# Attention scores of a hybrid decoder layer: fp32 products replaced by three products of (hi, lo) pairs

## The chip, the core and the metric

The kernel runs on one core of one Trainium2 chip. The metric is the device time of the whole program in microseconds (us). Work is spread over TensorE (PE in the profile; its weight loads have a row of their own, PEld), VectorE (DVE), ScalarE (ACT), GpSimd (POOL) and the DMA queues of SyncE (SP) and POOL.

## What is computed

One layer of a decoder trunk, 512 tokens of 1024 channels, all in fp32. Cut to the part that matters here:

```
h = RMSNorm(x);  [u | q | k | v] = h @ w_in            # 512 channels each
y_pool = pooling mixer on u, 4 groups, windows 2/4/8/16
# attention: 8 heads of 64 channels, blocks of 256 keys, top-3 past blocks + own block
l = q_head @ k_head.T * 64**-0.5 + bias(t - s);  l = where(allowed, l, -inf)
y_attn = softmax(l) @ v_head
x += RMSNorm(concat[y_pool, y_attn] @ w_out)
x += RMSNorm(conv-gated MLP of RMSNorm(x))             # 1024 -> 2 x 2816 -> 1024
x += (p @ w_ple) * sigmoid(x @ w_ple_gate)
```

With 512 tokens there are two blocks, so every past block is among the top three and the attention is plain causal attention.

## The kernel before, in words

Nearly all matrix products are done on pairs: an fp32 array is split into hi (rounded to the type fp32r) and lo (the rest, also fp32r), and a product is the sum of three fp32r matmuls into one bank, lo x hi, hi x lo and hi x hi. The helper `mm3` (lines 192 to 194) issues the three; `split` (lines 197 and 198) makes a pair, hi by an ACT copy and lo by a DVE subtraction. The class `_Weights` loads weights by SP's queue into two raw buffers and splits them into six pairs (lines 124 and 125), a few chunks ahead of their use, in the order that the program names them.

Two kinds of product are not on pairs. The transposes are fp32 matmuls against an identity. And the attention scores (`scores`, line 395) are plain fp32 matmuls: `query(hp)` and `key(hp)` project two heads at a time into one [128, 512] bank, lines 0 to 63 for the even head and 64 to 127 for the odd one, and ACT alone copies the bank to an fp32 tile, scaled by -1/8 for the queries (lines 380 and 385). For each head, `scores(h)` then issues four matmuls over the 64 lines of the head, one for each block of 128 queries, with 512, 384, 128 and 256 keys as moving columns (block i sees the keys up to its own end). They fill three banks with the tag `s`. DVE adds the bias and takes the minimum (line 401), ACT does the exponentials with the row sums (line 403), DVE scales by the reciprocals (lines 404 and 407).

The engines work their queues in program order (the schedule is manual). The attention part is one loop over the heads: some fills (a projection of 24 matmuls, or a small product `mix` of the pooling mixer, three matmuls), then `transposes(h)` (ten transposes of the softmax of head h, line 422; their three banks are split into the pair PT by ACT and DVE, lines 197 and 198), `scores(h + 1)`, and `values(h)` (eight fp32r matmuls, line 442, which read PT and V). So on TensorE the scores of the next head stand between the transposes of this head and its values, and the split of PT has the time of the scores to be done. After the last head's scores the fill is `out_part(0, 0)`, 15 matmuls of the output projection, and then `transposes(7)`.

POOL does the sums of the pooling mixer, small statistics, and issues its own DMAs: the bias table (`scr`, line 341, then `T`, line 483, which line 401 reads), gains, x, and later blocks of w_down.

The last line of the build creates the program with the default size of the ring in which POOL's DMAs put their descriptors (16384 bytes of each partition).

Of the kernel before, what the change touches and what calls it, by code (L numbers as in the profile page):

```python
# [17 lines left out]
F32 = mybir.dt.float32  # L18
F32R = mybir.dt.float32r
AF = mybir.ActivationFunctionType  # L20
ALU = mybir.AluOpType
# [3 lines left out]
P = 128  # L25
S = 512
# [5 lines left out]
DH = 64  # L32
# [107 lines left out]
def hybrid_layer(ctx, tc, x, p, rel_bias, g_mix_pre, g_mix_post, g_ffn_pre, g_ffn_post, w_in, w_pool,  # L140
                 pool_scale, w_out, w_up, conv_w, conv_b, w_down, w_ple, w_ple_gate, onehot, out):
    nc = tc.nc
    act, dve, pool, pe, sp = nc.scalar, nc.vector, nc.gpsimd, nc.tensor, nc.sync
# [10 lines left out]
    def bank(name, tag="mm"):  # L154
        return psum.tile([P, 512], F32, tag=tag, name=name, bufs=banks[tag])
# [34 lines left out]
    def mm3(o, st, mv, first, last, more=False):  # L190

        pe.matmul(o, st[1], mv[0], start=first, stop=False, skip_group_check=more)  # L192
        pe.matmul(o, st[0], mv[1], start=False, stop=False, skip_group_check=more)  # L193
        pe.matmul(o, st[0], mv[0], start=False, stop=last, skip_group_check=more)  # L194

    def split(pair, src):
        act.copy(pair[0], src)
        dve.tensor_sub(pair[1], src, pair[0].bitcast(F32))  # L198
# [77 lines left out]
    rows = early.tile([4 * NF + 4, P], F32, name="rows")  # L276
# [66 lines left out]
    ps = bank("rows", "pt")  # L343
# [12 lines left out]
    ap2 = at.enter_context(tc.tile_pool(name="attn2", bufs=1, reuse_waits="tile"))  # L356
# [10 lines left out]
    def project(name, tag="mm", n=3):  # L367
        w = W.take()
        ps = bank(name, tag)
        for k in range(KD):  # L370
            mm3(ps, [q[:, k, :] for q in w], h_moving(k), k == 0, k == KD - 1)
        W.ahead(n)
        return ps

    qT, kT, L = {}, {}, {}

    def query(hp):
        ps = project(f"q{hp}")
        qT[hp] = ap2.tile([P, S], F32, tag="qT", name=f"qT{hp}", bufs=2)
        act.mul(qT[hp], ps, -(DH ** -0.5))  # L380

    def key(hp):
        ps = project(f"k{hp}")
        kT[hp] = ap2.tile([P, S], F32, tag="kT", name=f"kT{hp}", bufs=2)
        act.copy(kT[hp], ps)

    place = {3: (0, 0, 768), 2: (1, 0, 384), 0: (1, 384, 0), 1: (2, 0, 128)}

    def scores(h):
        hp, e = divmod(h, 2)  # L390
        rows = slice(e * DH, (e + 1) * DH)
        bk = [bank(f"s{h}_{b}", "s") for b in range(3)]
        for i, (b, c, _) in place.items():
            n = (i + 1) * P
            pe.matmul(bk[b][:, c:c + n], qT[hp][rows, i * P:n], kT[hp][rows, :n], start=True, stop=True)  # L395
        L[h] = ap2.tile([P, 1280], F32, tag="L", name=f"L{h}", bufs=1)
        m = small.tile([P, 12], F32, tag="m", name=f"m{h}", bufs=2)
        for i, (b, c, o) in place.items():
            n = (i + 1) * P
            l = L[h][:, o:o + n]  # L400
            dve.tensor_tensor_reduce(out=l, in0=bk[b][:, c:c + n], in1=T[:, h, S - n:], scale=1.0, scalar=MASKED,
                                     op0=ALU.add, op1=ALU.min, accum_out=m[:, i:i + 1])
            act.activation(l, l, AF.Exp, bias=m[:, i:i + 1], scale=-1.0, accum_out=m[:, 4 + i:5 + i])
        dve.reciprocal(m[:, 8:], m[:, 4:8])
        for i, (b, c, o) in place.items():
            l = L[h][:, o:o + (i + 1) * P]
            dve.tensor_scalar_mul(l, l, m[:, 8 + i:9 + i])
# [78 lines left out]
    def y_stationary(t, k):  # L486
        return [q[:, k, t * P:(t + 1) * P] for q in yT]

    yb = {}
    part = (4, 5, 0, 1, 6)  # L490
    query(0)
    query(1)
    key(0)
    key(1)
    split(wp, wpool)
    scores(0)
    fills = {0: [lambda: pool_in(0)], 1: [lambda: pool_in(1)],
             2: [lambda: query(2), lambda: pool_out(0)],
             3: [lambda: query(3), lambda: key(2), lambda: pool_out(1)],
             4: [lambda: key(3)], 5: [lambda: pool_in(2)],  # L500
             6: [lambda: pool_in(3)]}
    after = {1: lambda: pool_mid(0), 2: lambda: pool_mid(1), 6: lambda: pool_mid(2)}
    for h in range(H - 1):
        for f in fills[h]:
            f()
        transposes(h)
        scores(h + 1)
        values(h)
        if h in after:
            after[h]()  # L510
# [77 lines left out]
    for k in range(2):  # L588
        ps = bank(f"trp{k}", "pt")
# [121 lines left out]
    for fb in range(1, NF // 2):  # L711
        for post in (gate_post, value_post):
            for f in (2 * fb, 2 * fb + 1):
                ps = project(f"{post.__name__[:4]}{f}", tags[u % 5])
# [162 lines left out]
```

## Time and profile before

| | us |
|---|---|
| median of 3 runs | 609.24 (608.72 to 611.42) |
| the profiled execution | 606.27 |
| its span, first to last instruction | 604.5 |
| TensorE busy in the span | 596.9 (99%) |
| VectorE, ScalarE, GpSimd busy | 397.9, 280.2, 180.6 |
| mean granted TensorE clock | 0.999 |

The span is the time from the first to the last instruction of the profiled execution; the execution's own time is 1.77 us longer. The profiled execution is 2.97 us faster than the median of the three timed runs, so a sum made against the trace is carried over to the median as a difference. A matmul's duration in the profile reaches beyond the start of the next one, since matmuls overlap in the array; what a matmul costs the engine is read from the starts of neighbours.

### The profile page before, as it was taken

How to read it: one execution, taken by the hardware profiler on the slowest of the kernel's cores; microseconds unless marked ns; L12 is line 12 of the kernel's file. 1: busy time of each engine (PE TensorE's matmuls, PEld its weight loads, DVE VectorE, ACT ScalarE, POOL GpSimd, SP SyncE). 2: the span in 40 equal slices, each digit the busy share in tenths (PEclk: the TensorE clock that was granted, in tenths of full speed). 3: DMA queues.
4: the chain of work that ended last, by engine and by line, in shares of the span. 5: the costliest groups of instructions: out<-in, count | busy, mean ns of one | idle time of the engine just before them, and what ended most of it. 6: DMA issues, size and time to landing. Idle time of an engine off the chain costs nothing.

```text
span 604.5 us, 7363 instructions
## 1 busy us (share of the span) xinstructions
PE 596.9 (99%) x2800; PEld 490.0 (81%) x2800; DVE 397.9 (66%) x552; ACT 280.2 (46%) x457; POOL 180.6 (30%) x198
## 2 busy tenths in 40 slices
PE   8999999999999999999999999999999999999997
PEld 5788777777888988888888888888888788888876
DVE  4732665777478668857766874654787786787432
ACT  5532655664454434413432342442565666657320
POOL 2300230045215446565646944214310000002000
PEclk9999999999999999999999999999999999999999
DMA  8676203023560696686777534224174577661311
GB/s 291 196 254 226 70 3 107 30 71 105 190 223 6 225 332 214 246 304 222 265 279 275 212 139 141 70 81 128 69 244 157 194 258 248 209 223 51 105 53 53
DMA packets 56492, 102.36 MB, mean 169 GB/s; under 512 B 2963, under 2 KB 32495, under 8 KB 55048
## 3 DMA queue, kind: packets, MB, share of 16 engines
q1 hardware_dynamic: 48344, 67.71, 34.1%
q0 software_dynamic: 8112, 34.17, 14.9%
q8 instruction: 22, 0.36, 0.3%
q14 instruction: 14, 0.11, 0.1%
HBM read 86.12 MB, written 18.37 MB: 173 GB/s over the span
## 4 chain that ended last, share of the span: by engine, by line
PE 94%; DMA 2%; DVE 1%; ACT 1%; issue 1%; SPq 1%; DVEq 0%; ACTq 0%
PE gate L192 6%; PE valu L192 6%; PE valu L194 6%; PE gate L194 6%; PE gate L193 6%; PE valu L193 6%; PE d L192 6%; PE d L194 5%; PE d L193 5%; PE s L395 3%; PE y L192 2%; PE y L193 2%; PE y L194 2%; PE g L193 2%; PE g L194 2%; PE g L192 2%
## 5 line engine op out<-in xcount | busy, mean ns | idle before, releaser
L125 DVE TENSOR_TENSOR wl<-raw,wh 128x1024 fp32r<-128x1024 f32 (+1 forms) x120 | 149.4, 1252 | 35.0 <-ACT wh L124 34.4
L124 ACT CAST wh<-raw 128x1024 fp32r<-128x1024 f32 (+1 forms) x120 | 120.6, 1021 | 24.4 <-DMA raw<-in_w_down 7.5
L679 POOL TENSOR_TENSOR b<-b 128x512 f32<-128x512 f32 x44 | 67.4, 1541 | 12.3 <-DMA b<-in_w_down 10.5
L192 PE MATMUL gate<-hT,wl 128*128 128x512 f32 x160 | 62.3, 389 | 0.0
L193 PE MATMUL gate<-hT,wh 128*128 128x512 f32 x160 | 62.3, 389 | 0.0
L194 PE MATMUL gate<-hT,wh 128*128 128x512 f32 x160 | 62.2, 389 | 0.0
L192 PE MATMUL valu<-hT,wl 128*128 128x512 f32 x160 | 62.2, 389 | 0.0
L193 PE MATMUL valu<-hT,wh 128*128 128x512 f32 x160 | 62.2, 389 | 0.0
L194 PE MATMUL valu<-hT,wh 128*128 128x512 f32 x160 | 62.2, 389 | 0.0
L192 PE MATMUL d<-wh,ml 128*128 128x512 f32 x154 | 60.0, 390 | 0.6 <-DVE ml L198 0.6
L194 PE MATMUL d<-wh,mh 128*128 128x512 f32 x154 | 59.9, 389 | 0.0
L193 PE MATMUL d<-wl,mh 128*128 128x512 f32 x154 | 59.9, 389 | 0.0
L618 ACT ACTIVATE c<-gate,cols 128x512 f32<-128x512 f32 x20 | 15.5, 777 | 67.7 <-PE gate L194 67.7
L619 DVE SCALAR_TENSOR_TENSOR c<-gate,cols,c 128x511 f32<-128x511 f32 x20 | 15.0, 748 | 36.3 <-ACT c L618 36.2
L631 ACT ACTIVATE sq<-sq 128x512 f32<-128x512 f32 x22 | 13.9, 632 | 50.2 <-DVE sq L630 50.2
L463 POOL TENSOR_TENSOR u<-u 128x512 f32<-128x512 f32 x10 | 11.3, 1134 | 80.8 <-ACT u L459 80.4
L194 PEld LDWEIGHTS gate<-hT,wh 128*128 128x128 f32 x160 | 30.0, 188 | 6.3
L194 PEld LDWEIGHTS valu<-hT,wh 128*128 128x128 f32 x160 | 30.0, 188 | 6.3
L193 PEld LDWEIGHTS valu<-hT,wh 128*128 128x128 f32 x160 | 30.0, 188 | 6.2
L192 PEld LDWEIGHTS valu<-hT,wl 128*128 128x128 f32 x160 | 30.0, 188 | 6.2
L193 PEld LDWEIGHTS gate<-hT,wh 128*128 128x128 f32 x160 | 30.0, 188 | 6.2
L192 PEld LDWEIGHTS gate<-hT,wl 128*128 128x128 f32 x160 | 30.0, 188 | 6.2
(200 smaller groups left out, 1286.0 us busy)
## 6 DMA issues: line engine op xcount, KB each, us to landing
raw<-in_w_up SPq DMA_DIRECT2D x22, 1024.0 KB, 5.3
b<-in_w_down POOLq DMA_DIRECT2D x22, 512.0 KB, 5.4
tsum<-b POOLq DMA_DIRECT2D x11, 1024.0 KB, 4.2
raw<-tsum SPq DMA_DIRECT2D x20, 512.0 KB, 5.1
raw<-in_w_down SPq DMA_DIRECT2D x15, 512.0 KB, 5.4
raw<-in_w_in SPq DMA_DIRECT2D x6, 1024.0 KB, 8.4
raw<-in_w_out SPq DMA_DIRECT2D x4, 1024.0 KB, 5.0
raw<-in_w_ple_gate SPq DMA_DIRECT2D x4, 1024.0 KB, 5.1
```

Source lines behind the costliest of these rows:

```text
L124: self.nc.scalar.copy(pair[0], view)
L125: self.nc.vector.tensor_sub(pair[1], view, pair[0].bitcast(F32))
L192: pe.matmul(o, st[1], mv[0], start=first, stop=False, skip_group_check=more)
L193: pe.matmul(o, st[0], mv[1], start=False, stop=False, skip_group_check=more)
L194: pe.matmul(o, st[0], mv[0], start=False, stop=last, skip_group_check=more)
L395: pe.matmul(bk[b][:, c:c + n], qT[hp][rows, i * P:n], kT[hp][rows, :n], start=True, stop=True)
L463: pool.tensor_tensor(out=nxt[:, 16:], in0=src[:, 16:], in1=src[:, 16 - (1 << lvl):16 + S - (1 << lvl)], op=ALU.add)
L618: act.activation(c0, pg, AF.Identity, bias=cw[:, 3, f:f + 1], scale=cw[:, 2, f:f + 1])
L619: dve.scalar_tensor_tensor(c0[:, 1:], pg[:, :S - 1], cw[:, 1, f:f + 1], c0[:, 1:], op0=ALU.mult, op1=ALU.add)
L631: act.activation(sq, sq, AF.Tanh)
L679: pool.tensor_tensor(out=b[:, o, :], in0=b[:, i0, :], in1=b[:, i1, :], op=ALU.subtract)
```

## The change

Queries and keys are split into (hi, lo) pairs when they leave PSUM: ACT still writes hi (now fp32r), and DVE gets one more instruction for each of the four query tiles (line 381 of the changed kernel) and each of the four key tiles (line 198, through `split`). `scores` calls `mm3` on the 64 lines of the head, so that each of its four matmuls becomes three fp32r ones. The pairs need twice the room of the single tiles (four tags of two buffers, 2 KB of each partition apiece), and the descriptor ring is set to 4096 bytes of each partition.

```diff
     def query(hp):
         ps = project(f"q{hp}")
-        qT[hp] = ap2.tile([P, S], F32, tag="qT", name=f"qT{hp}", bufs=2)
-        act.mul(qT[hp], ps, -(DH ** -0.5))
+        hi, lo = qT[hp] = [ap2.tile([P, S], F32R, tag=f"q{c}", name=f"q{c}{hp}", bufs=2) for c in "hl"]
+        act.mul(hi, ps, -(DH ** -0.5))
+        dve.scalar_tensor_tensor(lo, ps, -(DH ** -0.5), hi.bitcast(F32), op0=ALU.mult, op1=ALU.subtract)
 
     def key(hp):
         ps = project(f"k{hp}")
-        kT[hp] = ap2.tile([P, S], F32, tag="kT", name=f"kT{hp}", bufs=2)
-        act.copy(kT[hp], ps)
+        kT[hp] = [ap2.tile([P, S], F32R, tag=f"k{c}", name=f"k{c}{hp}", bufs=2) for c in "hl"]
+        split(kT[hp], ps)
...
             n = (i + 1) * P
-            pe.matmul(bk[b][:, c:c + n], qT[hp][rows, i * P:n], kT[hp][rows, :n], start=True, stop=True)
+            mm3(bk[b][:, c:c + n], [q[rows, i * P:n] for q in qT[hp]], [q[rows, :n] for q in kT[hp]], True, True)
...
-    nc = bacc.Bacc("TRN2", target_bir_lowering=False, num_devices=1)
+    nc = bacc.Bacc("TRN2", target_bir_lowering=False, num_devices=1, dynamic_dma_scratch_size=4096)
```

In the order of TensorE the change shows where a head's scores stand, between the transposes of the head before (pt) and that head's values (o). These are the rows before, at the scores of head 3; s are the score banks, kT and qT the key and query tiles:

```order
L422 MATMUL pt_2_811<-ident,L_725 128x128 x3
L395 MATMUL s_0_817<-kT_544,qT_480 128x512
L395 MATMUL s_1_818<-kT_544,qT_480 128x384
L395 MATMUL s_1_818<-kT_544,qT_480 128x128
L395 MATMUL s_2_819<-kT_544,qT_480 128x256
L442 MATMUL o_839<-PT_409,V 128x512
```

And these are the rows of the changed kernel at the scores of head 4 (kh, kl, qh, ql are the pairs; its lines after 381 are one further down):

```order
L423 MATMUL pt_2_987<-ident,L_866 128x128 x3
L192 MATMUL s_0_993<-kh_964,ql_823 128x512
L193 MATMUL s_0_993<-kl_965,qh_822 128x512
L194 MATMUL s_0_993<-kh_964,qh_822 128x512
L192 MATMUL s_1_994<-kh_964,ql_823 128x384
L193 MATMUL s_1_994<-kl_965,qh_822 128x384
L194 MATMUL s_1_994<-kh_964,qh_822 128x384
L192 MATMUL s_1_994<-kh_964,ql_823 128x128
L193 MATMUL s_1_994<-kl_965,qh_822 128x128
L194 MATMUL s_1_994<-kh_964,qh_822 128x128
L192 MATMUL s_2_995<-kh_964,ql_823 128x256
L193 MATMUL s_2_995<-kl_965,qh_822 128x256
```

Four matmuls of a head have become twelve, in the same place; nothing else on TensorE has moved.

On VectorE the added subtraction of the last key tile stands directly ahead of the split of PT on which the values of head 4 wait. Before (wl is the lo half of a weight chunk):

```order
L451 TENSOR_TENSOR yT_89<-d_981,t_978 64x512
L125 TENSOR_TENSOR wl_1010<-raw_788,wh_1009 128x1024
L198 TENSOR_TENSOR PT_409<-pt_0_1015,PT_408 128x512
L198 TENSOR_TENSOR PT_409<-pt_1_1022,PT_408 128x384
L198 TENSOR_TENSOR PT_409<-pt_2_1028,PT_408 128x384
```

Now:

```order
L452 TENSOR_TENSOR yT_89<-d_1035,t_1032 64x512
L125 TENSOR_TENSOR wl_1064<-raw_820,wh_1063 128x1024
L198 TENSOR_TENSOR kl_1068<-k_1038,kh_1067 128x512
L198 TENSOR_TENSOR PT_409<-pt_0_1071,PT_408 128x512
L198 TENSOR_TENSOR PT_409<-pt_1_1078,PT_408 128x384
L198 TENSOR_TENSOR PT_409<-pt_2_1084,PT_408 128x384
```

One instruction has come in ahead of the three splits.

## Rows read from the trace of the kernel before

**Rows 1.** The page's first part (busy us of each engine, share of the span, instructions) and the row of the granted TensorE clock in 40 slices, in tenths of full speed.

```profile
PE 596.9 (99%) x2800; PEld 490.0 (81%) x2800; DVE 397.9 (66%) x552; ACT 280.2 (46%) x457; POOL 180.6 (30%) x198
...
PEclk9999999999999999999999999999999999999999
```

**Rows 2.** The waits of TensorE's matmuls over the whole span: what waited, for what, us in total, times, longest. The view has four more rows: one of 1.4 us at the very start, before the first weights have come, and three of 0.3 us and less.

```profile
PE d L192 <- DVE ml L198: 0.6, 1, 0.6
PE tr L233 <- DVE hT L198: 0.4, 1, 0.4
```

**Rows 3.** The timeline of TensorE's matmuls from the last transposes of head 0 through the scores of head 1 to the first two values of head 0. Columns: start, us until the last of the row has ended, engine, line, operation, out<-in, shape, how many the row takes together. The rows come from narrow windows, so the counts overlap: a row's start is that of its first matmul.

```profile
68.60 0.27 PE L422 MATMUL pt<-ident,L 128*128 128x128 f32 x1
...
68.81 0.69 PE L395 MATMUL s<-kT,qT 64*128 64x512 f32 x1
...
69.34 0.91 PE L395 MATMUL s<-kT,qT 64*128 64x512 f32 x2
...
69.77 0.81 PE L395 MATMUL s<-kT,qT 64*128 64x384 f32 x2
...
70.41 0.60 PE L395 MATMUL s<-kT,qT 64*128 64x128 f32 x3
...
70.63 0.59 PE L395 MATMUL s<-kT,qT 64*128 64x256 f32 x2
...
70.85 0.38 PE L395 MATMUL s<-kT,qT 64*128 64x256 f32 x1
...
71.16 0.50 PE L442 MATMUL o<-PT,V 128*128 128x512 f32 x1
...
71.50 0.58 PE L442 MATMUL o<-PT,V 128*128 128x512 f32 x2
```

**Rows 4.** The timeline of TensorE's weight loads in the same stretch, with the same columns; in brackets, the idle time before the row.

```profile
68.80 0.29 PEld L395 LDWEIGHTS s<-kT,qT 64*128 64x128 f32 x2 [0.17 <-issue]
69.34 0.19 PEld L395 LDWEIGHTS s<-kT,qT 64*128 64x128 f32 x1 [0.24 <-issue]
```

**Rows 5.** The timeline of TensorE's matmuls at the values of head 7, which follow a product of the pooling mixer and not scores. All of them are fp32r: two with 512 columns (the rows begin with the second of them), then two with 384, then four with 256.

```profile
150.82 0.56 PE L442 MATMUL o<-PT,V 128*128 128x512 f32 x2
...
151.04 0.33 PE L442 MATMUL o<-PT,V 128*128 128x384 f32 x1
...
151.22 0.46 PE L442 MATMUL o<-PT,V 128*128 128x384 f32 x2
...
151.39 0.52 PE L442 MATMUL o<-PT,V 128*128 128x256 f32 x3
...
151.51 0.52 PE L442 MATMUL o<-PT,V 128*128 128x256 f32 x3
```

**Rows 6.** The timeline of TensorE's matmuls from the last transpose of head 7 to the second matmul of the output projection that follows.

```profile
146.35 0.27 PE L422 MATMUL pt<-ident,L 128*128 128x128 f32 x1
...
146.69 0.39 PE L193 MATMUL y<-wl,yT 128*128 128x512 f32 x1
```

**Rows 7.** The timelines of ACT, DVE and PE around the third key tile (`key(2)`): its copy out of PSUM, a result of the mixer on DVE, the DVE part of the split of PT, the scores of head 4 and the first values of head 3.

```profile
105.14 0.59 ACT L385 COPY kT<-k 128x512 f32<-128x512 f32 x1 [3.91 <-PE k L194]
...
106.54 0.75 DVE L480 SCALAR_TENSOR_TENSOR yT<-mix,cols,yT 128x512 fp32r<-128x512 f32 x1 [4.05 <-ACT yT L479]
107.21 1.61 DVE L198 TENSOR_TENSOR PT<-pt,PT 128x512 fp32r<-128x512 f32 x3
...
106.80 2.42 PE L395 MATMUL s<-kT,qT 64*128 64x512 f32 x8
109.16 0.50 PE L442 MATMUL o<-PT,V 128*128 128x512 f32 x1
```

**Rows 8.** The same around the fourth key tile (`key(3)`): its copy on ACT, the DVE part of the split of PT, the first values of head 4.

```profile
116.22 0.59 ACT L385 COPY kT<-k 128x512 f32<-128x512 f32 x1 [2.17 <-PE k L194]
...
117.33 1.62 DVE L198 TENSOR_TENSOR PT<-pt,PT 128x512 fp32r<-128x512 f32 x3 [1.34 <-ACT PT L197]
...
119.56 0.74 PE L442 MATMUL o<-PT,V 128*128 128x512 f32 x2
```

**Rows 9.** The timelines at the last head: the DVE scaling of its softmax, the last matmul of `out_part(0, 0)`, and the weight loads of `transposes(7)` from the second on.

```profile
143.41 1.95 DVE L407 TENSOR_SCALAR L<-L,m 128x512 f32<-128x512 f32 x4
...
144.96 0.39 PE L194 MATMUL y<-wh,yT 128*128 128x512 f32 x1
...
145.41 0.42 PEld L422 LDWEIGHTS pt<-ident,L 128*128 128x128 f32 x4 [0.31 <-DVE L L407]
```

**Rows 10.** DVE at head 0: the split of the mixer's weights ahead of the softmax, the first bias row, the scaling.

```profile
60.92 0.69 DVE L198 TENSOR_TENSOR wp<-wpool,wp 128x512 fp32r<-128x512 f32 x1 [3.78 <-ACT wp L197]
61.53 0.68 DVE L401 CUSTOM_DVE_ANT_0 L<-s,T 128x512 f32<-128x512 f32 x1
...
64.80 1.27 DVE L407 TENSOR_SCALAR L<-L,m 128x512 f32<-128x512 f32 x4
```

**Rows 11.** PE at the start of `transposes(0)`, and two of the page's DMA issues of POOL's queue: KB of one, us from issue to landing; then the issue of the second on POOL's timeline.

```profile
67.62 0.38 PE L422 MATMUL pt<-ident,L 128*128 128x128 f32 x2
...
scr<-line POOLq DMA_DIRECT2D x1, 2560.0 KB, 16.6
...
T<-scr POOLq DMA_DIRECT2D x1, 2048.0 KB, 9.9
...
40.59 0.95 POOL L483 DMA_DIRECT2D T<-scr  x1 [14.87 <-DMA scr<-line]
```

## The prediction

> **What bounds the kernel now.** I read the page's first part first. TensorE is busy 99% of the span, its clock is at full speed in every slice, and VectorE, the next engine, has a third of the span free [rows 1]. A busy TensorE could still be one that waits between matmuls, so I read its waits next. Apart from the start of the program the longest is 0.6 us, in the down projection, and in the whole attention part no matmul's start is put down to another engine [rows 2]. So a microsecond less of TensorE's own work in that part is a microsecond of the whole, unless something off the engine then ends last. The question is thus what one head's scores cost TensorE now, what twelve fp32r products will cost, and at which head another engine stands close behind.
>
> For the first part I read the timeline by starts. From the first score matmul to the first matmul of the values it is 68.81 to 71.16, 2.35 us [rows 3]; it is 106.80 to 109.16 at head 4 [rows 7], and the same at the other heads. Each fp32 product appears as two records. One record takes 0.43 us for 512 columns (69.34 to 69.77), 0.32 for 384 (69.77 to 70.41 for two), 0.11 for 128 (70.41 to 70.63 for two) and 0.22 for 256 [rows 3]. That is some 1,280 columns, twice, at two clock periods of 2.4 GHz each, 2.13 us. The remaining 0.2 us stands at the ends. The first record takes 0.53 instead of 0.43, and the last one 0.31 (70.85 to 71.16) instead of 0.22 [rows 3].
>
> **What the change removes and adds on TensorE.** An fp32r matmul of the same width is a single record: 0.22 us for 512 columns (150.82 to 151.04), 0.175 for 384 (151.04 to 151.39 for two), 0.12 for 256 (151.39 to 151.51) [rows 5]. The first one after the scores takes 0.34 (71.16 to 71.50) [rows 3]: 0.12 more, for a weight load that nothing covers. I take that for the first product of the scores too, since their first record carries a like surcharge now, and I leave the 0.09 at the end, since 64 lines give way to 128 there as before.
>
> No row shows an fp32r matmul with 128 columns. The bounds are 0.06, half of the 256-column one, and 0.22, if the narrow one cost as much as the two records of the fp32 product. I take 0.11: two weight loads that follow each other without a matmul between them start 0.10 apart (0.29 us for the two, 0.19 for one [rows 4]), each product loads weights anew, and so a product cannot follow faster than that, however narrow it is. It is also what one fp32 record of this width takes.
>
> One head's scores are then 0.34 + 2 x 0.22 for 512 columns, 3 x 0.175 for 384, 3 x 0.11 for 128, 3 x 0.12 for 256, and 0.09 at the end: 2.085 us instead of 2.35. That is **0.265 us less for each head**: three passes for four, of which the narrow products and the fixed part of each instruction take half back.
>
> **What it adds elsewhere, and what covers it.** DVE gets eight more instructions: four like the mixer's from PSUM, 0.75 us [rows 7], and four subtractions of 512 columns at 0.69 [rows 10], some 5.8 us in all, beside DVE's 206 us of idle time. ACT has the same instructions as before. What matters is who waits for them, and there are three places.
>
> At the third key tile the copy on ACT ends at 105.73. The lo half takes DVE until about 106.45; DVE was idle until 106.54, and the product that reads it is the second of head 4's scores, from 106.80 on [rows 7]. It costs nothing; the cover is 0.35 us, and any lateness beyond that is paid in full.
>
> At the fourth key tile the lo half runs from about 116.84 to 117.53, directly ahead of the split of PT, which began at 117.33 [rows 8]. The split is pushed by 0.2 and ends at 119.15 instead of 118.95. The values of head 4 began at 119.56 and will want to begin at 119.30, and they need only the first third of the split at their start (about 118.2). At head 3 the split ends at 108.82 and the values will come at 108.90 [rows 7]. So the shorter scores still cover the split; about 0.9 us would have to go before the first values wait.
>
> At head 0 the second key tile pushes the mixer's split, and with it the softmax, by about 0.2 us: its scaling ends at 66.3 instead of 66.07 [rows 10], and the transposes will come at 67.35 instead of 67.62 [rows 11]. A full projection of 5.4 us covers this, as at every head but the last.
>
> At the last head this cover is 15 matmuls, 3.4 us, and it is used up: the scaling on DVE ends at 145.36, TensorE was free at 145.19, and the second transpose's load already waited until 145.41 [rows 9]. DVE's chain to that point starts from the split of PT of the head before and not from the scores (its first bias step stands right behind that split in DVE's order), so it does not get shorter. TensorE will come 0.265 us earlier and wait as much longer. **Head 7 gives nothing**, and the sum is 7 x 0.265 = 1.85 us.
>
> The larger pairs and the smaller ring move the tiles in SBUF, which changes for which released tiles POOL's loads of x and w_down wait. I cost this at nothing, as TensorE shows no wait for any of them [rows 2]. The ring itself matters for two DMAs. The bias goes through `scr` (16.6 us from issue to landing) and `T` (issued at 40.59, 9.9 us), so T has landed at 50.5 [rows 11], and DVE first reads it at 61.53 [rows 10]. A ring that slowed these would have 11 us to use up first. I cost it at nothing as well.
>
> **The sum.** The profiled execution takes 606.27 us, 1.77 of it outside the span; 606.27 - 1.85 = 604.4. That execution is 2.97 us faster than the median of the runs, so against the median it is 609.24 - 1.85 = **607.4 us**, 0.3% less. About 0.5% (3.05 us) is what a measurement of this kernel can tell from no change, so I call this no change.
>
> **The rivals.** *Narrow products at the rate of the wide ones* (0.06 us): 0.15 more for each head, 0.415 x 7 = 2.9 us, 606.3. For it: the 256-column products come near the rate of their columns. Against it: the 0.10 between two loads. If the last head's chain also gave way, it would be 3.3 us.
>
> *The ends go away.* If the surcharges at both ends (0.09 of idle time and 0.12 of uncovered load, twice) belonged to fp32 and not to the 64 lines, another 0.42 us would go from each head: 0.685 x 7 = 4.8 us, 604.4. Against it: where fp32 transposes over 128 lines give way to fp32r ones, the second of these starts 0.34 after the last transpose [rows 6], which is 0.11 + 0.23 and no surcharge.
>
> *The products are not what they say.* If the 128-column ones cost 0.22, a head takes 0.065 more than now, and 7 of them 0.5 us: 609.7. If every product over 64 lines cost an fp32 record, a head would take 3 x (0.43 + 0.32 + 0.11 + 0.22) + 0.2 = 3.45, 1.1 more, and eight heads 8.8 us: 618.0. Against the latter: the same type runs at 0.22 over 128 lines [rows 5].
>
> *Weight loads come into the open*, which ends on the other side. The place is the twelve products of a head, which all use the same 64 lines of the array. If each load stood between its neighbours as the first one does, 12 x 0.12 would come on top of the streams, 3 x (0.22 + 0.175 + 0.12 + 0.06), and 0.09: 3.25 us, 0.9 more than now, and 7.2 us for eight heads: 616.4. It decides from the third uncovered load of a head on, since each costs 0.12 and the gain is 0.265. Against it: in the scores of now the loads start with the matmul ahead of them (69.34 in both views), and a matmul follows the next one after exactly its columns [rows 3, 4]. The Trainium skill, "TensorE: Matmul & The Clock Gate", Part 3 (The mechanism), says of packed matmuls that a weight load overlaps with matmuls in flight only where the two address different rows of the array; by that rule the time would be this rival's 616.4 us, and the trace, with loads over the same 64 lines hidden behind 0.43 us records, does not agree.
>
> *The ring delays the bias.* If both DMAs took twice as long, T would land at 77.0, and head 0's softmax, 15 us late with 1 us to spare, would cost some 14 us: 623. It would have to be slower by 11 us before it cost anything.
>
> **How the numbers follow.** The forecast has 0.67, narrow products at full rate 0.13, ends that go 0.04, products that cost more 0.09 (0.07 the narrow ones, 0.02 all), open loads 0.04, the ring 0.03. The range goes from 605.6 to 609.9: it takes in the first and the narrow part of the third rival and, below, the half microsecond by which the fastest run before lies under its median. It leaves out 0.13. Faster by over 0.5% are the ends, and the part of the first rival that the last head or the spread takes over the line: 0.08. Slower by over 0.5% are all products at the fp32 price, open loads and the ring: 0.09. The rest, 0.83, is within 0.5%.
>
> **What would show it.** In the profile after, the scores of a head should take 2.0 to 2.15 us from their first start to the first values, with starts 0.22 to 0.23, 0.17 to 0.18, about 0.11 and 0.12 apart. The second transpose of head 7 should wait some 0.5 us for DVE instead of 0.3, and no other new wait of TensorE should exceed 0.2. DVE's busy time should rise by 5 to 6 us, ACT's not. The prediction is wrong if the 128-column products are far from 0.11 apart, if a load of the scores starts after the matmul ahead of it has ended, or if a wait for DVE appears ahead of head 4's scores or of any head's values.

## The result and the profile after

The changed kernel takes **605.3 us** (median of 5 executions, 604.84 to 605.99) beside 609.24 (607.21 to 611.42) for the kernel before in the same session: a ratio of 0.9935 [0.9907, 0.9963]. The forecast was 607.4, and its range ended 0.3 us higher than the result. The two profiled executions are 604.84 and 606.27 us (spans 603.1 and 604.5), so the traces account for 1.43 us, not for the 3.9 us between the medians. Where the other 2.5 us are is the main question of the experiments. The forecast called the change no change; the interval of the ratio ends below 1, so it is one, of 0.4 to 0.9%.

The first part of the page after, to be read against [rows 1]: TensorE has 1.9 us less to do, DVE 12 us more, where 5 to 6 were forecast. The eight new instructions take 0.69 us each, 5.5 in all, as forecast; the rest lies in instructions that the change doesn't touch, and DVE's busy time differs as much between profiles of one kind (397 to 404 us in the six with fp32 scores, 404 to 410 in the seven with all three products).

```profile
PE 595.0 (99%) x2832; PEld 494.5 (82%) x2832; DVE 410.0 (68%) x560; ACT 279.9 (46%) x457; POOL 184.3 (31%) x198
```

TensorE's waits over the whole span after (columns as in [rows 2]). The second row is new; it stands at the transposes of head 7.

```profile
PE d L192 <- DVE ml L198: 0.7, 1, 0.7
PE pt L423 <- DVE L L408: 0.5, 1, 0.5
PE tr L233 <- DVE hT L198: 0.4, 1, 0.4
```

TensorE's timeline after at the scores of head 1, which answers to [rows 3]; columns as there.

```profile
68.60 0.50 PE L192 MATMUL s<-kh,ql 64*128 64x512 f32 x1
68.94 0.39 PE L193 MATMUL s<-kl,qh 64*128 64x512 f32 x1
69.17 0.39 PE L194 MATMUL s<-kh,qh 64*128 64x512 f32 x1
69.41 0.33 PE L192 MATMUL s<-kh,ql 64*128 64x384 f32 x1
...
69.93 0.22 PE L192 MATMUL s<-kh,ql 64*128 64x128 f32 x1
69.99 0.27 PE L193 MATMUL s<-kl,qh 64*128 64x128 f32 x1
70.10 0.27 PE L194 MATMUL s<-kh,qh 64*128 64x128 f32 x1
70.21 0.33 PE L192 MATMUL s<-kh,ql 64*128 64x256 f32 x1
70.39 0.28 PE L193 MATMUL s<-kl,qh 64*128 64x256 f32 x1
70.51 0.28 PE L194 MATMUL s<-kh,qh 64*128 64x256 f32 x1
70.71 1.09 PE L443 MATMUL o<-PT,V 128*128 128x512 f32 x4
```

Read by starts: 0.34 for the first product, 0.23 for the next two, 0.17 for each with 384 columns, 0.06, 0.11 and 0.11 for those with 128, then 0.17 (70.21 to 70.39; the rows are rounded), 0.12 and 0.20 up to the values. The scores of a head take 2.11 us (68.60 to 70.71) in place of 2.35.

TensorE's weight loads in the same stretch (columns as in [rows 4]): the load for the second 384-column product starts at 69.41, with the matmul ahead of it, and the others likewise or 0.05 to 0.11 later; only the first load of the head (68.60) starts together with its own matmul and not ahead of it.

```profile
68.60 0.18 PEld L192 LDWEIGHTS s<-kh,ql 64*128 64x128 f32 x1 [0.17 <-issue]
...
69.41 0.18 PEld L193 LDWEIGHTS s<-kl,qh 64*128 64x128 f32 x1
...
69.93 0.18 PEld L193 LDWEIGHTS s<-kl,qh 64*128 64x128 f32 x1
70.04 0.19 PEld L194 LDWEIGHTS s<-kh,qh 64*128 64x128 f32 x1
70.15 0.19 PEld L192 LDWEIGHTS s<-kh,ql 64*128 64x128 f32 x1
```

Set against the trace before, the values of head 0 start 0.45 us earlier (71.16 to 70.71) and those of head 6 2.01 us earlier (140.36 to 138.35): 0.26 from head to head, of which 0.24 stand in the scores themselves and the rest between them. Behind head 7's transposes only 1.50 us are left (the first product there, 146.37 to 144.87). Half a microsecond is given back at that one place. Two timelines show how, DVE's of the kernel before around the splits of PT of heads 5 and 6:

```profile
127.73 1.16 DVE L198 TENSOR_TENSOR PT<-pt,PT 128x512 fp32r<-128x512 f32 x2 [1.88 <-ACT PT L197]
...
132.53 2.21 DVE L407 TENSOR_SCALAR L<-L,m 128x512 f32<-128x512 f32 x4
...
136.22 2.36 DVE L125 TENSOR_TENSOR wl<-raw,wh 128x1024 fp32r<-128x1024 f32 x2
138.61 0.69 DVE L198 TENSOR_TENSOR PT<-pt,PT 128x512 fp32r<-128x512 f32 x1
```

and the same after, with TensorE at the transposes of head 7 under it:

```profile
126.23 1.62 DVE L198 TENSOR_TENSOR PT<-pt,PT 128x512 fp32r<-128x512 f32 x3 [1.52 <-ACT PT L197]
...
131.03 2.20 DVE L408 TENSOR_SCALAR L<-L,m 128x512 f32<-128x512 f32 x4
...
134.71 2.36 DVE L125 TENSOR_TENSOR wl<-raw,wh 128x1024 fp32r<-128x1024 f32 x2
137.10 1.16 DVE L198 TENSOR_TENSOR PT<-pt,PT 128x512 fp32r<-128x512 f32 x2
...
141.90 1.91 DVE L408 TENSOR_SCALAR L<-L,m 128x512 f32<-128x512 f32 x4
```

```profile
142.96 0.40 PE L194 MATMUL y<-wh,yT 128*128 128x512 f32 x1
143.83 1.29 PE L423 MATMUL pt<-ident,L 128*128 128x128 f32 x10 [0.47 <-DVE L L408]
144.87 0.48 PE L192 MATMUL y<-wh,yT 128*128 128x512 f32 x1
```

The split of head 5 is the last thing on DVE that waits for TensorE (1.88 and 1.52 us of idle time ahead of it, ended by ACT's half of the split, which reads the transposes); it comes 1.50 us earlier. From there to head 7's scaling DVE waits only for ACT's exponentials, whose own inputs come from DVE, and every row of it comes 1.50 or 1.51 us earlier, no more: the split of head 6 stands behind two weight splits that keep DVE busy until 138.58 (now 137.07), whenever TensorE is done. So neither head 7's shorter scores nor head 6's reach the end: six heads count, not seven.

### The profile page after: what moved, and what is told of

The parts are those of the page before. It is cut to its first block, busy times and chain, and to the rows that moved or that the text cites. A ratio compares the mean times of both kernels' runs of the same rounds, so it can differ in the third digit from the quotient of the medians.

```text
span 603.1 us, 7432 instructions
## 1 busy us (share of the span) xinstructions
PE 595.0 (99%) x2832; PEld 494.5 (82%) x2832; DVE 410.0 (68%) x560; ACT 279.9 (46%) x457; POOL 184.3 (31%) x198
## 4 chain that ended last, share of the span: by engine, by line
PE 93%; DVE 3%; ACT 2%; issue 1%; POOL 1%; DVEq 0%; POOLq 0%
PE gate L192 6%; PE valu L194 6%; PE gate L194 6%; PE valu L192 6%; PE gate L193 6%; PE valu L193 6%; PE d L192 6%; PE d L193 5%; PE d L194 5%; PE g L193 2%; PE g L194 2%; PE y L194 2%; PE y L192 2%; PE g L192 2%; PE y L193 2%; PE tr L233 2%
## 5 line engine op out<-in xcount | busy, mean ns | idle before, releaser
L125 DVE TENSOR_TENSOR wl<-raw,wh 128x1024 fp32r<-128x1024 f32 (+1 forms) x120 | 152.7, 1279 | 22.7 <-ACT wh L124 22.1
L680 POOL TENSOR_TENSOR b<-b 128x512 f32<-128x512 f32 x44 | 71.2, 1628 | 10.5 <-DMA b<-in_w_down 8.8
L222 POOL TENSOR_SCALAR rd<-msd 128x1 f32<-128x1 f32 x4 | 3.1, 784 | 106.5 <-ACT M L217 106.5
```

The source lines that it names most:

```text
L125: self.nc.vector.tensor_sub(pair[1], view, pair[0].bitcast(F32))
L222: pool.tensor_scalar(r, ms, add, None, op0=ALU.add)
L680: pool.tensor_tensor(out=b[:, o, :], in0=b[:, i0, :], in1=b[:, i1, :], op=ALU.subtract)
```

## The experiments

The kernels ran in three sessions (e, g, h), each on one chip and beside runs of the kernel before, whose medians there were 607.33 (35 executions), 607.15 (20) and 607.37 (19), with 606.18 and 611.38 as the extremes. Ratios are to these runs, with their 95% intervals; they are not the ratios of the medians.

**The base, the ring, the tiles (e1 to e4).** e1 is the kernel before and e4 the changed one, unedited. e2 has one line of the change, e3 the changed kernel with a ring of twice the size, which moves its tiles again:

```diff
 e2 (kernel before)
-    nc = bacc.Bacc("TRN2", target_bir_lowering=False, num_devices=1)
+    nc = bacc.Bacc("TRN2", target_bir_lowering=False, num_devices=1, dynamic_dma_scratch_size=4096)
 e3 (changed kernel)
-    ... dynamic_dma_scratch_size=4096)
+    ... dynamic_dma_scratch_size=8192)
```

> The kernel before, unchanged, against itself: what its own executions spread over, with the span and clock of each. If the 2.5 us that the change gained beyond the 1.4 us of the two traces lie in the measurement of the kernel before (chance of the chip or the moment), its median comes out near its trace, 606 to 607, here. If they belong to the program, its executions lie at 607 to 611 again, ratio 1.00, and a trace of a slow one shows where the 1 to 5 us stand.

> The kernel before with the ring at 4096 bytes and nothing else: fp32 scores, all tiles 12 KB lower. Theory A (the scores alone act, the rest is spread): same as before, 607 to 611, scores 2.35 us a head. Theory B (ring or place of the tiles removes slow executions): 606.0 to 606.8, 2.5 us less than before, with no difference in the scores. Theory C (the ring costs something that the scores hide): above before by 0.5 us or more.

> The changed kernel with a ring of 8192 bytes, all tiles 4 KB higher than in the change. If the size of the ring acts, the time lies between: 606 to 608. If only the scores act, or the place of the tiles does not matter, it is the change's 605.3 within 0.6 us. Scores 2.11 us a head either way.

> The changed kernel unchanged, on the same chip as the three others, so that they can be compared: 604.8 to 606.0 as at first, ratio 0.9935 if the kernel before has its slow executions here too, 0.9975 (1.4 to 1.8 us) if it has not.

| | median us (12 executions) | lowest, highest | ratio |
|---|---|---|---|
| e1, before | 607.43 | 606.16, 610.7 | 0.9992 [0.9969, 1.0015] |
| e2, ring alone | 606.95 | 606.12, 608.17 | 0.9982 [0.9964, 1.0] |
| e3, pairs, ring 8 KB | 606.83 | 605.62, 607.84 | 0.9973 [0.9951, 0.9995] |
| e4, the change | 605.61 | 604.8, 605.99 | 0.9956 [0.9937, 0.9975] |

With more executions the median of the kernel before is 607.3, not 609.24, and the change is worth 1.7 us between medians (by the interval of the ratio 1.5 to 3.8). e2 lies between the ranges of its theories A and B. The executions of the kernel before are not one level with noise: of the 35, seven lie at 606.2 to 606.6, seven at 610.4 to 611.3, and the rest in steps between, while e4 stays within 1.2 us. The profiled execution of e1 (608.18) shows one of the steps. Its rows of SP's issue of a w_up block, of ACT's cast of it, and of the transposes of the second norm on TensorE:

```profile
165.74 0.37 SPq L101 DMA_DIRECT2D raw<-in_w_up  x1
...
173.88 1.05 ACT L124 CAST wh<-raw 128x1024 fp32r<-128x1024 f32 x1 [5.43 <-DMA raw<-in_w_up]
...
184.32 1.10 PE L233 MATMUL tr<-ident,h2n 128*128 128x128 f32 x8 [1.86 <-DVE h2n L570]
```

The block is issued as in the other trace of this kernel (165.83), but is cast 2.5 us later than there:

```profile
171.38 1.05 ACT L124 CAST wh<-raw 128x1024 fp32r<-128x1024 f32 x1 [2.84 <-DMA raw<-in_w_up]
```

The cast stands in ACT's queue ahead of squares (line 217) that the second norm needs, so a late block delays the norm and in the end TensorE, by 1.86 us. Up to there e1 is as early as the first trace, so this wait is all of its distance. What is in flight just ahead of that block are POOL's loads of x and p, 2.5 MB. In the kernel before they wait for the last product of the mixer; after the change the first of these tiles lies elsewhere and waits for the values of head 7 (the second gain's DMA, before and after):

```profile
156.55 0.53 POOL L211 DMA_DIRECT2D g_ffn_pre<-in_g_ffn_pre  x1 [9.38 <-PE mix L194]
157.07 1.05 POOL L538 DMA_DIRECT2D x<-in_x  x2
```

```profile
150.84 0.53 POOL L211 DMA_DIRECT2D g_ffn_pre<-in_g_ffn_pre  x1 [4.93 <-PE o L443]
151.36 1.05 POOL L539 DMA_DIRECT2D x<-in_x  x2
```

In e2 they are issued from 152.9 on and no execution is above 608.2; in e3 from 158.5 on, the second-norm transposes wait 0.6 us again, and the median is 1.2 above e4. (That wait is not all of it: see the starts below.)

**The tiles without the scores, and the scores without the early loads (g1, g2).** g1 gives the fp32 tiles the size of the pairs and takes the small ring; g2 puts the loads of the changed kernel back behind the last mixer product.

```diff
 g1 (kernel before, ring 4096)
-        qT[hp] = ap2.tile([P, S], F32, tag="qT", name=f"qT{hp}", bufs=2)
+        qT[hp] = ap2.tile([P, 2 * S], F32, tag="qT", name=f"qT{hp}", bufs=2)[:, :S]
...
 g2 (changed kernel)
+    hold = small.tile([P, 1], F32, tag="hold", name="hold", bufs=1)
+    pool.tensor_copy(out=hold, in_=yT[1][:, 3, :1].bitcast(F32))
     g_pre = gains(op_, g_ffn_pre, "g_ffn_pre")
```

> The kernel before with the ring of 4096 bytes and with query and key tiles of twice the size, of which only the first half is used: every tile and every DMA descriptor stands where the changed kernel has it, and the scores are still fp32. If the scores alone made the change (0.25 us less for each of seven heads), the executions of this kernel lie as the changed kernel's do, 1.4 to 1.8 us higher: about 606.4 and 607.3, median 606.9, none above 608.5, with x issued at 151 to 155 us and no wait of the h2n transposes for DVE. If the place of the tiles made the change, it comes to 605.6 to 606.0. If neither the ring nor the tiles do anything, it lies as before: median 607.3, a fifth of the executions above 610.

> The changed kernel with POOL's loads of the second gain, x and p held behind the last product of the mixer by a one-column copy of its result, as they stood before. If these loads, by delaying the first w_up block, make the slow executions, x is issued after 155.5 us, the cast of that block starts later than 170.5, the h2n transposes wait 0.5 to 2 us for DVE, and executions above 606.5 appear: median 606.0 to 607.0. If the moment of these loads does not matter, it lies as the changed kernel: 604.8 to 606.0, median 605.6. The scores stay at 2.11 us a head in both.

g1: 606.58 (606.22 to 608.28, 10 executions); x is issued at 152.77, no wait of these transposes shows, nothing is above 608.5. g2: 606.84 (606.13 to 607.73, 10), with 0.9981 [0.996, 1.0002]; seven of ten executions lie above 606.5. These medians jump between steps, and the ratio of g1 alone, 1.0003 [0.9993, 1.0013], shows no gain. So I take the means of all executions of a kind together (the interval is a bootstrap over them; sessions on different chips are pooled):

| | x from 151 to 153 us on | x from 157 us on |
|---|---|---|
| fp32 scores | e2, g1: 606.89 (606.61 to 607.20), 22 executions, none above 608.28 | before, e1: 607.89 (607.60 to 608.21), 86, of which 25 above 608.3 and 14 above 610 |
| pairs | the change: 605.54 (605.34 to 605.74), 23, none above 606.64 | e3, g2: 606.76 (606.47 to 607.07), 22, none above 607.84 |

Between the means, the scores are worth 1.1 to 1.35 us, and the column with the early loads, of which the diff says nothing, lies 1.0 to 1.2 lower (in medians, e2 0.4 and g1 0.6 below the kernel before). That these 1.0 to 1.2 belong to the loads is not shown, for the means hold something else as well: executions of one kernel differ from the first 20 us on. By 22 us TensorE is 1.1 us behind the first trace of the changed kernel in e4 and 2.0 in e3, and 2.0 behind the first trace of the kernel before in h2 (the kernel before with an edit at head 7, below). The scores of head 0 in the kernel before and in h2:

```profile
59.68 2.42 PE L395 MATMUL s<-kT,qT 64*128 64x512 f32 x8
```

```profile
61.57 1.77 PE L395 MATMUL s<-kT,qT 64*128 64x512 f32 x4
```

No load at 151 us can have caused this. Added to 606.2, the lowest time of the kernel before, it gives 607.3 and 608.2. Around these two, from 606.7 to 608.4, lie 47 of the 86 executions and 12 of the 22 of e2 and g1. That they are slow starts is an estimate from these three traces. e3's profiled execution is 2.71 us behind the changed kernel's first trace: 2.01 by 22 us, 0.7 at the transposes. What speaks for the loads is the tail: 23 of the 86 executions lie above 608.4, none of the 45 with early loads. Against it: none of the 22 of e3 and g2, with late loads, is above 607.84 (609.2 with the 1.4 us of the scores added), while 14 of the 86 are above 610. The late loads alone have not brought back executions as slow as these.

A size missed in g2: the transposes wait 0.25 us in its profile, not 0.5 to 2 (the cast starts at 172.21, as expected late). Of the 2 us by which that execution is slower than the one profiled of the changed kernel, 0.81 is already there at 21 us, 0.4 comes at these transposes, and some 0.5 comes between 150 and 180 us, where its 512-column products follow 0.233 instead of 0.229 apart; for that no cause was found.

**A larger dose (h1).** The kernel before, with the loads of x and p moved behind POOL's first `s` of the output projection.

```diff
-    for t in range(NT):
-        pool.dma_start(X[t], x[t * P:(t + 1) * P, :])
...
-    pool.dma_start(pin, p.rearrange("(t q) c -> q t c", q=P))
...
         s0.append(s)
+        if t == 0:
+            for i in range(NT):
+                pool.dma_start(X[i], x[i * P:(i + 1) * P, :])
+            pool.dma_start(pin, p.rearrange("(t q) c -> q t c", q=P))
```

> The kernel before with POOL's loads of x and p issued one small POOL instruction later, behind the first sum of the output projection's squares: about 163 to 166 us instead of 157 to 160. If the slow executions of the kernel before come from these 2.5 MB delaying the w_up block that is loaded at 165.8, the delay is now the rule: the cast of that block starts at 174 us or later in every execution, the h2n transposes wait 2 us or more for DVE, and the median is 608.5 to 612, with no execution under 607.5. If the executions at 610 to 611 (granted clock 0.997) are such a wait together with a late rise of the clock at the start, executions at that level come up in a third or more. If the moment of these loads does not matter, it lies as before: 606.2 to 611.4, median 607.2.

613.53 (611.38 to 614.71, 6 executions), 1.0079 [1.0054, 1.0103], a little above the range expected. In its profile the loads are issued from 164.06 to 167.1, and the block behind them (issued at 167.05) is cast 10.5 us after its issue:

```profile
177.58 1.05 ACT L124 CAST wh<-raw 128x1024 fp32r<-128x1024 f32 x1 [7.82 <-DMA raw<-in_w_up]
...
188.01 1.97 PE L233 MATMUL tr<-ident,h2n 128*128 128x128 f32 x8 [3.67 <-DVE h2n L571]
```

All six executions are as slow as the slowest of the kernel before. Of the 8.4 us by which the profiled one is behind the first trace of that kernel, 1.2 are there from the start, 0.6 is a wait for p itself, which this edit adds, 3.8 come at these transposes, and 2.8 with a fall of the clock behind them (last section). So such a collision can make these times; that it makes them in the kernel before is not shown. In a row, each from one profile (x: POOL's first issue; block: from SP's issue of the w_up block to its cast; wait: TensorE's at those transposes):

| | x, us | block, us | wait, us |
|---|---|---|---|
| changed kernel | 151.4 | 5.25 | none |
| g1 | 152.8 | 5.25 | none |
| before, first trace | 157.1 | 5.55 | none |
| before, e1 | 157.0 | 8.14 | 1.86 |
| g2 | 158.3 | 6.88 | 0.25 |
| e3 | 158.5 | 6.89 | 0.62 |
| h2 | 158.8 | 5.29 | none |
| h1 | 164.1 | 10.52 | 3.67 |

With x issued by 153 the block takes 5.0 to 5.3 us, in all eight profiles; from 157 to 159 on it takes 5.3 to 8.1, in five. h2 has late loads and no late block:

```profile
172.83 1.05 ACT L124 CAST wh<-raw 128x1024 fp32r<-128x1024 f32 x1 [2.58 <-DMA raw<-in_w_up]
```

The two traces of the kernel before differ by 2.6 us with the same issue times. So a late block shows only in profiles with late loads, but not in all of them. Why one execution collides and the other doesn't, the runs don't show.

**DVE's chain at the last heads (g3, h3, g4, h2).** g3 and h3 are the same kernel, the changed one with 3 matmuls more ahead of transposes(7); h2 is the kernel before with that edit; h4 is the changed kernel once more, beside h2 and h3.

```diff
     out_part(0, 0, part, True, False)
+    out_part(1, 0, part[:1], True, False)
     transposes(H - 1)
-    out_part(1, 0, part, True, False)
+    out_part(1, 0, part[1:], False, False)
```

> The changed kernel with the first 3 of the 15 matmuls of out_part(1, 0) moved ahead of transposes(7). If head 7's part of the gain is held back by DVE's softmax chain alone, TensorE's wait of 0.5 us there goes, the transposes of head 7 start when the extra 0.7 us of matmuls end, and the time is 0.4 to 0.55 us less than the changed kernel's 605.6: about 605.1, executions near 604.35 and 605.4. If something later takes it back (the split of PT of head 7, whose cover is 0.7 us shorter), the values of head 7 wait for DVE instead and the time stays at 605.6.

> The changed kernel with the cover at head 7, a second time and beside the changed kernel on the same chip: by the first look executions at 604.2 and 605.0 to 605.3, median 604.2 to 604.8, which is 0.6 to 0.8 us under the changed kernel's. If the first look was luck with the rise of the clock at the start, the medians differ by less than 0.3.

> The changed kernel as it is, for the comparison with its neighbours on this chip: executions at 604.8 to 604.9 and 605.5 to 606.0, median 605.6, none above 606.1. If its narrow spread so far was luck, executions above 607 turn up as in the kernel before.

> The kernel before with the first 3 matmuls of out_part(1, 0) moved ahead of transposes(7). In its trace the transposes of head 7 lose 0.2 to 0.4 us to DVE, so by the theory (head 7 gives the change nothing because of DVE's chain) the best executions go from 606.2 to about 605.85, and the change with this cover gains 8 x 0.25 = 2.0 us over this kernel, not 1.4. If the cover itself is worth as much in both kernels (0.7 us), head 7's loss has nothing to do with the change: best executions at 605.5, and 1.4 from the change as without cover.

g3: 604.2 (604.19 to 604.98, 5 executions), 0.9961 [0.9948, 0.9974] against the kernel before. h3: 604.9 (604.17 to 606.04, 6), 0.9945 [0.9923, 0.9968], beside h4 with 605.77 (605.51 to 606.64, 6), 0.9961 [0.9939, 0.9983]. So g3 comes out 0.9 below its forecast, h3 0.1 above its range, and h4 has one execution, 606.64, above the 606.1 that it was to keep under. The wait at the transposes of head 7 is gone, and the products follow without a gap:

```profile
143.68 0.40 PE L194 MATMUL y<-wh,yT 128*128 128x512 f32 x1
143.91 1.25 PE L423 MATMUL pt<-ident,L 128*128 128x128 f32 x10
144.92 0.47 PE L192 MATMUL y<-wh,yT 128*128 128x512 f32 x1
```

From one profile to the other TensorE gains 0.67 us at this place (h4 to h3) or 0.68 (after to g3), read from the products behind it on both sides, more than the 0.40 to 0.55 expected: the gap of 0.64 beyond the 0.23 of a product (142.96 to 143.83 above) goes whole, not only the 0.47 that the view calls a wait. In the kernel before the same edit is worth 0.19 in the trace, and its best execution goes from 606.18 to 606.0, less than the 0.35 expected (median 606.99, 0.9981 [0.9961, 1.0]). Between h2 and h3, both with cover, TensorE's distance grows from 1.87 us ahead of head 0's scores to 3.86 at the values of head 6 and is the same behind the transposes of head 7: 1.99, that is the gain of all eight heads, and none of it is given back there. The kernel of g3 and h3 beats both.

g4 leaves the product lo x hi out of the scores (a part of the computation).

```diff
-            mm3(bk[b][:, c:c + n], [q[rows, i * P:n] for q in qT[hp]], [q[rows, :n] for q in kT[hp]], True, True)
+            qs, ks = [q[rows, i * P:n] for q in qT[hp]], [q[rows, :n] for q in kT[hp]]
+            pe.matmul(bk[b][:, c:c + n], qs[0], ks[1], start=True, stop=False)
+            pe.matmul(bk[b][:, c:c + n], qs[0], ks[0], start=False, stop=True)
```

> The changed kernel without the product lo x hi in the scores (two products for each block instead of three, a part of the computation left out). If a microsecond less of TensorE's own work in the scores of heads 0 to 6 is a microsecond of the whole, and head 7 gives nothing, each head takes 0.60 to 0.65 us less (2.11 to about 1.48) and the whole 4.2 to 4.6 us less: about 601.2. DVE's wait at transposes(7) grows from 0.5 to 1.1. If the split of PT on DVE is next behind, the values of some heads wait for DVE and the whole gets only 2.5 to 4 us less: 601.6 to 603.1.

603.12 (602.48 to 604.41, 4 executions): the second theory, and a little worse. Beside e4, whose first 20 us are like its own, TensorE is 5.00 us earlier at the last score product (139.30 to 134.30), but only 2.35 behind the transposes of head 7. TensorE's longest wait:

```profile
PE o L445 <- DVE PT L198: 1.5, 1, 1.5
```

It is the split of head 6, the one behind the two weight splits. After the wait TensorE's granted clock (the column after POOL's) fell for about 3 us, which the values of head 6 paid:

```profile
134.00:136.00 2.00, 0.58 (x5) 0.37 (x3) 1.97 (x3) 0.00 (x0) 1.92 (x2) 0.94 0.00 0
136.00:138.00 2.00, 1.89 (x6) 1.70 (x7) 2.00 (x8) 0.37 (x1) 1.84 (x3) 0.50 0.64 163
138.00:140.00 2.00, 2.00 (x9) 1.77 (x9) 0.68 (x7) 1.98 (x9) 1.85 (x3) 0.70 0.93 362
```

The wait takes 1.6 us of the lead and the slower clock another 1.4. Of the wait, 0.84 us comes with one of the two weight splits, which takes 2.06 us instead of 1.22 in a stretch in which POOL adds (132.80 to 136.23); whether the one slows the other no run shows. So a further microsecond in the scores is not a microsecond of the whole: DVE is next, at head 6.

## Why the prediction was right on the mechanism and wrong on the time

- **The scores: right.** Forecast 2.085 us a head and 0.265 less than before; measured 2.11, 0.24 less in the scores and 0.26 from head to head. The three 128-column products took 0.06 + 0.11 + 0.11 instead of 0.33, and the first 256-column one behind them 0.17 instead of 0.12: two small misses that cancel. The reason given for 0.11, that a product can't follow faster than two loads do, does not hold for the first of the three. The first product (0.34) and the end (0.20, 0.09 over the 0.11 or 0.12 of its neighbours) kept their surcharge.
- **The rival of open weight loads: refuted.** Eleven of the twelve loads of a head run while an earlier matmul is in flight. The Trainium skill, "TensorE: Matmul & The Clock Gate", Part 3 (The mechanism), says that a load overlaps with matmuls in flight only where their row groups differ; the same section also names a background weight buffer as a way for a load to run ahead. These loads use the same 64 lines as the matmuls that they overlap, with 0.06 to 0.23 us from product to product, so the trace disagrees with the first statement and not with the second.
- **The covers at the third and fourth key tile: right.** No scores and no values wait for DVE; the DVE work of the new lo halves is paid by idle time. The sign "DVE's busy time should rise by 5 to 6 us" missed (12).
- **Head 7: the wait was right (0.5), the count was not.** "DVE's chain to that point starts from the split of PT of the head before" is one step that failed, by 0.3 us: that split itself doesn't wait for TensorE, since DVE comes to it late from the weight splits. The chain starts at the split of head 5, so six heads count: 6 x 0.26 = 1.56 against 1.85. The traces differ by 1.50 behind head 7 and by 1.43 as a whole.
- **The base: the step on which the time failed.** "so against the median it is 609.24 - 1.85" carries a difference of TensorE's work over to a median of three executions, all of them 2.4 us or more above the profiled one, as if that distance were a constant of the kernel. With the two executions that came with the result the median of that session stays 609.24. The median of 86 later executions is 607.3. That is 1.9 of the 2.1 us by which the forecast missed: from 607.3 the same 1.85 would have given 605.5. Of five executions drawn from the 86, some 3 in 100 draws have a median of 609.24 or more, so the base was a rare draw, or something of that session; the runs don't show which. The distance that is left, from 606.3 to 607.3, is about that of a slower start (1.1 us), which the change doesn't touch: the changed kernel has the same two levels, 604.84 and 605.99.
- **The moved tiles at nothing: wrong, by a size that is not settled.** "TensorE shows no wait for any of them" is true of the one trace that was read, an execution at 606.27. In e1 TensorE does wait, 1.86 us behind x's loads, and the new place of the tiles issues these loads 6 us earlier. In medians the early loads go with 0.4 to 0.6 us less (e2, g1, without the scores), in means with 1.0 to 1.2, of which the starts have a part. Put together, 607.3 less 1.5 for six heads less 0.4 to 0.6 is 605.2 to 605.4, where 605.3 was measured and 605.6 and 605.8 in the later sessions.
- **The ring as a delay of the bias: rightly held unlikely.** e2 is no slower than the kernel before.

What stays open: why the block behind x's loads is late in some executions only; how much of the early loads' gain belongs to them and how much to the starts; whether the executions of e2 and g1 at 608.2 are slow starts, as h2's of 607.94 is; and, as no execution of the kernel before above 610 was profiled, whether those are a wait behind the loads, with or without the fall of the clock that h1 shows.

## What to carry to other kernels

Where the profiled execution lies well under the median, the difference is time too: take more executions, and profile a slow one, before a sum is carried over; here it was a slow start in one (h2) and a late weight block in another (e1), at nearly the same time in all. And ask of each tile that moves which loads it lets go earlier. A gain on the busiest engine counts up to the last place where another engine's queue waits for it; follow that queue back until an instruction has idle time ahead of it. Three matmuls of cover at the right place were worth 0.67 us, nearly half of what the change gave in the traces.

## What the runs showed of the hardware that was not expected

- **The clock after a wait.** In h1 the wait of 3.67 us costs more than itself. The granted clock (the column after POOL's) is 1.00 until the last microsecond of the wait and 0.50, the 1.2 GHz level, for 6 us behind it:

```profile
184.00:186.00 2.00, 0.34 (x2) 0.00 (x0) 1.97 (x2) 0.97 (x2) 0.00 (x0) 1.00 0.98 306
186.00:188.00 2.00, 0.00 (x0) 0.00 (x0) 1.03 (x3) 0.75 (x4) 1.57 (x4) 0.79 0.63 211
188.00:190.00 2.00, 1.99 (x9) 1.99 (x10) 1.91 (x3) 0.58 (x1) 0.38 (x1) 0.50 0.00 0
...
194.00:196.00 2.00, 2.00 (x10) 1.64 (x9) 0.54 (x1) 0.69 (x2) 0.39 (x2) 1.00 0.00 0
```

TensorE is 5.63 us behind the kernel before when it starts again and 8.41 when the clock is back: 2.8 us on top. The wait of 1.53 us in g4 has such a fall too; that of 1.86 us in e1 has none, and there TensorE keeps its distance of 1.93 us to the other trace of that kernel to the end.
- **The pace at the start differs from execution to execution.** The first value products of e4 follow 0.43 us apart, as the products of h1 do at a granted 0.50:

```profile
14.03 0.63 PE L193 MATMUL v<-wl,hT 128*128 128x512 f32 x1
14.45 0.63 PE L194 MATMUL v<-wh,hT 128*128 128x512 f32 x1
```

and those of the changed kernel's first trace, where products follow 0.23 apart, the full rate, which is there from 10.4 us on instead of 16.4 (17.6 in e3 and h2):

```profile
12.33 0.39 PE L193 MATMUL v<-wl,hT 128*128 128x512 f32 x1
12.55 0.39 PE L194 MATMUL v<-wh,hT 128*128 128x512 f32 x1
```

That alone is 1.1 us between two executions of one kernel (604.84 and 605.99), and it stays to the end. The pace is that of the 1.2 GHz level, but the granted clock reads 1.00 from 4 to 22 us in all these traces, so that the clock makes it is likely and not shown; TensorE is busy without a gap from 10 to 17 us in e4.
- **A 128-column fp32r product behind a wider one takes 0.06 us from its start to the next (69.93 to 69.99), the two behind it 0.11 each.** The loads start 0.11 apart there (69.93, 70.04, 70.15), so it is likely that they set the pace; no run tests it.
